# Output projection of a hybrid encoder layer as seven block products instead of eight, with split weight operands parked in DRAM

## The chip, the cores and the metric

The kernel runs on one core of one Trainium2 chip. Its time is the device time of one execution in microseconds (us). Five engines work side by side and meet at semaphores: TensorE (PE: matmuls and transposes), VectorE (DVE), ScalarE (ACT), GpSimd (POOL) and SyncE (SP). Transfers are issued from a queue of SP, ACT or POOL and are carried by sixteen DMA engines that all queues share. The tile framework orders each engine's instructions ahead of time; only TensorE's order is written out by hand in the stages described here.

## The reference

One layer of a bidirectional encoder: 512 tokens, model width 1024, float32.

```python
u = h @ w_in
z, xbc, dt_f_raw, dt_b_raw, q, k, v, gate_logits = jnp.split(u, ...)
y_ssd = ssd_branch(z, xbc, ...) @ w_proj_ssd        # (512, 2048) @ (2048, 1024)
y_att = attention_branch(q, k, v) @ w_proj_attn     # (512, 256) @ (256, 1024)
gates = jax.nn.sigmoid(gate_logits + b_gate).reshape(bsz, s, N_BRANCHES, D_MODEL)
mix = (gates[:, :, 0] * y_ssd + gates[:, :, 1] * y_att) @ w_out   # (512, 1024) @ (1024, 1024)
h = layer_norm(alpha * h + mix, ln1_g, ln1_b)
f = jnp.square(jax.nn.relu(h @ w_up)) @ w_down      # width 4096
h = layer_norm(alpha * h + f, ln2_g, ln2_b)
```

The change is about the product with `w_out`, and about what has to be ready around it.

## The kernel before

**Split operands.** Every float32 operand `r` of a large product is held as a high part `h` (a cast by ScalarE to the matmul type, line 109) and a low part `l = r - h` (a subtraction by VectorE, line 110). A product is then three matmuls into the same PSUM bank: high x high, high x low, low x high (`mm3`, lines 165 to 172).

**Weights.** `Stream` (lines 75 to 130) loads weight tiles of 128x1024 (512 KB) in the order of use into three raw buffers (`wraw`), from SP's queue, and splits each one just ahead of its use. A tile with a `hold` is split into a buffer of its own that stays (`wo` for the output projection, `wb` for the attention projection, `wu` for the first blocks of the up projection).

**Order of the stages.** The input projection and the scan over four groups of heads (to about 455 us); attention, with the first twelve half products of `w_proj_ssd` running between (to about 577 us); the last four half products, each followed by the attention projection and the gates of two blocks of 128 features (`proj_b`, lines 1072 to 1083, to 605 us); the output projection and the first norm (605 to 657 us); the up and down projections, already done as seven block products each; the last norm.

**The output projection.** `proj_b(d)` finishes the gated sum of feature block `d` for all 512 tokens and splits it into `mixh[d]` and `mixl[d]`. Eight PSUM banks hold the result: four token blocks of 128 by two column halves of 512. `out_mm(i, k, ...)` adds feature block `k` to token block `i`: two halves of three matmuls. Blocks `k` 0 to 3 run over all four token blocks with weights that stream in; `out_tail(i)` then does blocks 4 to 7 of one token block with the four tiles held in `wo`, adds the scaled input row `h1[i]` (two evictions, line 1182) and normalizes it (`layer_norm`, lines 1131 to 1140). While the later token blocks run, the finished ones are transposed for the up projection (`h1_transpose`). `up_first` is the first half of two up blocks and covers the norm of the last token block.

```python
    for k in range(4):
        w = ws.get(2)
...
        for i in range(4):
            out_mm(i, k, *w)
...
    out_tail(0)
    out_tail(1)
    out_tail(2)
    h1_transpose(0)
    out_tail(3)
```

**Buffers.** `yh`, `yl` (the split scan output) lie on the right side of the on-chip memory and are read until the last half product of `w_proj_ssd`; `h1` and what is allocated after it take their place. `wb` lies on the left side and is read until the last `proj_b`. A new buffer's first write waits for the last reader of what lay there.

Of the kernel before, what the change touches and what calls it, by code (L numbers as in the profile page):

```python
# [10 lines left out]
F32 = mybir.dt.float32  # L11
# [5 lines left out]
P = 128  # L17
# [29 lines left out]
def hybrid_layer_kernel(ctx: ExitStack, tc: tile.TileContext, t: dict, out: bass.AP):  # L47
# [18 lines left out]
    dr_w0 = dram.tile([S, 4], F32, name="dr_w0")  # L66

# [7 lines left out]
    class Stream:  # L75
        def __init__(self):
            self.srcs, self.raw, self.hl, self.n, self.end = [], {}, {}, 0, None

# [16 lines left out]
        def prep(self, i):  # L95
            if i < len(self.srcs) and i not in self.hl and (self.end is None or i < self.end):
                self.load(i)
                ap, width, hold = self.srcs[i]
                if hold and hold[0] not in held:
                    return  # L100
                r = self.raw[i]
                if hold:
                    h = held[hold[0]].tile([P, 1024], F32R, name=f"wh{i}", tag=f"h{hold[1]}", bufs=1)
                    l = held[hold[0]].tile([P, 1024], F32R, name=f"wl{i}", tag=f"l{hold[1]}", bufs=1)
                else:
                    h = wp.tile([P, 1024], F32R, name=f"wh{i}", tag="wh", bufs=2)
                    l = wp.tile([P, 1024], F32R, name=f"wl{i}", tag="wl", bufs=2)
                with tc.high_priority(PRIO):
                    a = act.copy(h[:, :width], r[:, :width])  # L109
                    v = dve.tensor_sub(l[:, :width], r[:, :width], f32(h[:, :width]))  # L110
# [510 lines left out]

    late = [None]
# [16 lines left out]
    def ssd(g):  # L639
# [104 lines left out]
        for pr in range(4):  # L744
# [14 lines left out]
            pool.tensor_add(be[:, 0, P:S - P], be[:, 0, P:S - P], be[:, 1, P:S - P])  # L759
# [57 lines left out]
    a_order = [(d, i) for i in range(2) for d in range(3)] + [(d, i) for d in range(3, 8) for i in range(2)]  # L817
    for n, (d, i) in enumerate(a_order):
        if n == 12:
            for q in range(2):  # L820
                ws.add(t["w_pa"][q], hold=("wb", q))
        ws.add(t["w_ps"][d, i])
        if n >= 12:
            ws.add(t["w_out"][n - 8], hold=("wo", n - 12))
    for k in range(4):
        ws.add(t["w_out"][k])
        if 0 < k <= NU:
            ws.add(t["w_up"][k - 1], hold=("wu", k - 1))
# [3 lines left out]
    mixa = [mx.tile([P, S], F32, name=f"mixa{d}", tag="mix", bufs=9) for d in range(8)]  # L832
    mixl = []
    ath = [mx.tile([P, S], F32R, name=f"ath{i}") for i in range(2)]
    atl = [mx.tile([P, S], F32R, name=f"atl{i}") for i in range(2)]
# [13 lines left out]
    aq = at_ctx.enter_context(tc.tile_pool(name="aq", bufs=1, side="right", reuse_waits="tile"))  # L849

    def attention():
# [21 lines left out]
        b12 = ap.tile([P, 8, P], F32, name="b12")  # L873
# [11 lines left out]
        b0 = aq.tile([P, 4, 256], F32, name="b0")  # L885
# [143 lines left out]
        def merge(i):  # L1029
# [3 lines left out]
            act.copy(ath[i], ac)  # L1033
            dve.tensor_sub(atl[i], ac, f32(ath[i]))

        todo = []
# [35 lines left out]
    def proj_b(d):  # L1072
# [7 lines left out]
        dve.tensor_add(gb, gb, mixa[d])  # L1080
        mixl.append(mx.tile([P, S], F32R, name=f"mixl{d}", tag="mix", bufs=9))
        act.copy(mixh[d], gb)
        dve.tensor_sub(mixl[d], gb, f32(mixh[d]))
# [9 lines left out]
    mixh = [mh.tile([P, S], F32R, name=f"mixh{d}") for d in range(8)]  # L1093
    held["wo"] = mp.enter_context(tc.tile_pool(name="wop", bufs=1, reuse_waits="tile"))
    wb_ctx = ExitStack()
    held["wb"] = wb_ctx.enter_context(tc.tile_pool(name="wbp", bufs=1, reuse_waits="tile"))
    wb = [ws.get() for _ in range(2)]
    wo, wu = [], []
    for d, i, bs in ((6, 0, (0, 1)), (6, 1, (2, 3)), (7, 0, (4, 5)), (7, 1, (6, 7))):
# [3 lines left out]
        for q in bs:  # L1103
            proj_b(q)
    wb_ctx.close()
    yp_ctx.close()
# [10 lines left out]
    hf_ctx = ExitStack()  # L1117
    hf = hf_ctx.enter_context(tc.tile_pool(name="hf", bufs=1, side="right", reuse_waits="tile")).tile([P, KT, S], F32, name="hf")
# [34 lines left out]
    pso_b = [(6, 7), (5, 2), (3, 4), (0, 1)]  # L1153
    pso_t = [bank(n, f"ps_o{n}") for n in range(8)]
    pso = [[pso_t[n] for n in b] for b in pso_b]

    def out_mm(i, k, wh, wl):
        ts_ = slice(i * P, (i + 1) * P)
        for c in range(2):
            cs = slice(c * 512, (c + 1) * 512)  # L1160
            mm3(pso[i][c], [(mixh[k][:, ts_], mixl[k][:, ts_])], [(wh[:, cs], wl[:, cs])], first=(k == 0), last=(k == KT - 1))
# [3 lines left out]
    for k in range(4):  # L1165
        w = ws.get(2)
        if 0 < k <= NU:
            wu.append(ws.get(1))
        for i in range(4):
            out_mm(i, k, *w)  # L1170
        if k == 0:
            g1 = load_ln(held["wu"], 0)
        dma.dma_start(h1[k], t["x"][k * P:(k + 1) * P, :])

    def out_tail(i):
        for k in range(4):
            out_mm(i, 4 + k, *wo[k])
            if i == 3 and k == 1:
                h1_transpose(1)
        for c in range(2):  # L1180
            cs = slice(c * 512, (c + 1) * 512)
            dve.scalar_tensor_tensor(h1[i][:, cs], h1[i][:, cs], 2.0 * ALPHA, pso[i][c], op0=ALU.mult, op1=ALU.add)
        layer_norm(h1[i], g1, 0, f"a{i}")
# [20 lines left out]
    def up_first(i):  # L1204
        pre.append(bank((6, 7, 5, 2)[i], f"ps_u0_{i}"))
# [26 lines left out]
    def up_block(ch, b):  # L1232
# [16 lines left out]
    LO, HI = slice(0, 256), slice(256, 512)  # L1249
# [408 lines left out]
def _layout(a):  # L1658
# [21 lines left out]
    o["w_out"] = c(a["w_out"].reshape(KT, P, D))  # L1680
# [21 lines left out]
```

## Time and profile before

| what | before |
|---|---|
| median of 3 runs | 985.0 us (984.65 to 985.14) |
| the profiled execution | 984.4 us, its span 982.7 us |
| TensorE busy | 972.9 us (99%) |
| VectorE busy | 806.5 us (82%) |
| ScalarE busy | 607.2 us (62%) |
| GpSimd busy | 76.2 us (8%) |
| moved by DMA | 155.94 MB, 159 GB/s over the span |
| granted TensorE clock | 0.999 |

The profile is one execution. The span runs from its first to its last instruction; times in its views are counted from the span's start. A row of the timeline gives the start, the duration, the engine, the line of the kernel, the operation and the names of the tiles, written tile first, and how many instructions are merged into the row; a bracket names the idle time before it and what ended it. A row of stretches gives, for each engine, the busy time and the number of instructions in it, then the granted clock, the mean busy share of the sixteen DMA engines, and GB/s. Matmul durations overlap, so a busy TensorE isn't a TensorE at its peak.

### The profile page before, as it was taken

What the parts mean: (1) busy time and instruction counts of PE and PEld (TensorE: products, weight loads), DVE (VectorE), ACT (ScalarE), POOL (GpSimd) and SP (SyncE); (2) the same over time, 40 slices, a digit from 0 to 9 for tenths busy, and PEclk for the clock granted to TensorE, in tenths of its full rate; (3) what the DMA queues carried; (4) which work ended last, traced back from release to release, by engine and by line L of the source; (5) the groups of instructions that cost most, each with busy time, mean ns of one, the idle gap of its engine ahead of it and who ended that gap; (6) DMA issues with size and microseconds to landing.
All of it is one profiled execution on the core that took longest, in us unless ns stands there. A gap on an engine that the chain in (4) does not pass through costs nothing.

```text
span 982.7 us, 14783 instructions
## 1 busy us (share of the span) xinstructions
PE 972.9 (99%) x5447; PEld 835.1 (85%) x5447; DVE 806.5 (82%) x1235; ACT 607.2 (62%) x1149; POOL 76.2 (8%) x79
## 2 busy tenths in 40 slices
PE   9999999999999999999999999999999999999997
PEld 6988888888888888788778888899989998989986
DVE  7986998798998899997798258498898898898757
ACT  6664796469856995694775344147666666656620
POOL 0100100120011101202000000000200110110000
PEclk9999999999999999999999999999999999999999
DMA  9666476335652485474773248313953854671322
GB/s 355 152 146 171 127 199 199 97 116 153 214 151 90 149 243 147 123 234 140 252 237 111 79 149 313 127 44 125 242 148 131 213 129 171 176 169 44 110 83 86
DMA packets 57992, 155.94 MB, mean 159 GB/s; under 512 B 7488, under 2 KB 10432, under 8 KB 57664
## 3 DMA queue, kind: packets, MB, share of 16 engines
q1 hardware_dynamic: 53072, 139.04, 43.9%
q0 software_dynamic: 4560, 15.44, 8.6%
q8 instruction: 43, 0.70, 0.3%
q10 hardware_dynamic: 288, 0.52, 0.1%
q14 instruction: 29, 0.24, 0.1%
HBM read 128.25 MB, written 12.44 MB: 143 GB/s over the span
## 4 chain that ended last, share of the span: by engine, by line
PE 86%; DVE 8%; ACT 3%; DMA 2%; issue 1%; DVEq 0%; SPq 0%; ACTq 0%
PE ps_pa L159 9%; PE ps_z L159 8%; PE ps_x L159 8%; PE ps_x L1341 8%; PE ps_z L1341 4%; PE ps_k L159 3%; PE ps_g L159 3%; PE ps_q L159 3%; PE ps_pX L169 2%; PE ps_pX L170 2%; PE ps_pX L171 2%; PE ps_y L1341 2%; PE ps_vX L351 2%; PE ps_u L159 2%; PE ps_pZ L169 2%; PE ps_pZ L170 2%
## 5 line engine op out<-in xcount | busy, mean ns | idle before, releaser
L110 DVE TENSOR_TENSOR wl<-wraw,wh 128x1024 fp32r<-128x1024 f32 x103 | 129.7, 1265 | 57.4 <-ACT wh L109 42.2
L109 ACT CAST wh<-wraw 128x1024 fp32r<-128x1024 f32 x103 | 107.2, 1045 | 73.9 <-PE ps_o L171 13.2
L1457 DVE TENSOR_TENSOR cl<-wq_B,ch 128x1024 fp32r<-128x1024 f32 x42 | 51.2, 1220 | 14.8 <-ACT ch L1456 14.3
L1456 ACT CAST ch<-wq_B 128x1024 fp32r<-128x1024 f32 x42 | 44.1, 1050 | 24.0 <-PE ps_pX L171 16.6
L159 PE MATMUL ps_pa<-yh,wh 128*128 128x512 f32 x128 | 51.7, 404 | 0.0
L1425 POOL DMA_DIRECT2D wq_B<-wq_B x24 | 20.6, 856 | 391.2 <-DMA wq_B<-in_w_dn_dram 225.4
L159 PE MATMUL ps_g<-xh,wh 128*128 128x512 f32 x128 | 50.6, 396 | 0.0
L159 PE MATMUL ps_z<-xh,wh 128*128 128x512 f32 x128 | 50.4, 393 | 0.0
L159 PE MATMUL ps_g<-xl,wh 128*128 128x512 f32 x128 | 49.9, 390 | 0.0
L159 PE MATMUL ps_z<-xl,wh 128*128 128x512 f32 x128 | 49.9, 389 | 0.0
L159 PE MATMUL ps_pa<-yl,wh 128*128 128x512 f32 x128 | 48.4, 393 | 0.0
L724 ACT ACTIVATE U<-bc,acr 128x128 f32<-128x128 f32 x128 | 42.3, 391 | 8.9 <-DMA bc<-dr_acr 7.7
L159 PE MATMUL ps_x<-xh,wh 128*128 128x512 f32 x120 | 47.2, 394 | 0.0
L159 PE MATMUL ps_x<-xl,wh 128*128 128x512 f32 x120 | 46.7, 389 | 0.0
L522 DVE SCALAR_TENSOR_TENSOR acc<-ps_x,vec,acc 128x510 f32<-128x510 f32 (+1 forms) x60 | 44.5, 742 | 0.7 <-ACT acc L520 0.3
L726 DVE SCALAR_TENSOR_TENSOR U<-bc,acr,U 128x128 f32<-128x128 f32 x128 | 43.2, 375 | 0.8 <-ACT U L724 0.8
L730 ACT ACTIVATE G<-cb,tok 128x128 f32<-128x128 f32 x128 | 41.7, 391 | 0.0
L169 PE MATMUL ps_pX<-ch,ah 128*128 128x512 f32 x96 | 37.6, 392 | 0.0
L170 PE MATMUL ps_pX<-cl,ah 128*128 128x512 f32 x96 | 37.6, 392 | 0.0
L171 PE MATMUL ps_pX<-ch,al 128*128 128x512 f32 x96 | 37.3, 389 | 0.0
L1450 ACT CAST ah<-r 128x1024 fp32r<-128x1024 f32 x21 | 22.1, 1053 | 20.6 <-PE ps_pX L170 14.3
L159 PE MATMUL ps_pa<-yh,wl 128*128 128x512 f32 x128 | 34.8, 392 | 0.0
(884 smaller groups left out, 2841.2 us busy)
## 6 DMA issues: line engine op xcount, KB each, us to landing
wraw<-in_w_in_dram SPq DMA_DIRECT2D x66, 512.0 KB, 3.8
bc<-dr_acr SPq DMA_DIRECT2D x64, 256.0 KB, 4.4
pr<-in_w_up_dram SPq DMA_DIRECT2D x28, 512.0 KB, 5.5
wq_B<-in_w_dn_dram SPq DMA_DIRECT2D x24, 512.0 KB, 4.5
wq_B<-wq_B POOLq DMA_DIRECT2D x24, 512.0 KB, 4.7
be<-dr_ear SPq DMA_DIRECT2D x32, 256.0 KB, 5.1
wraw<-in_w_ps_dram SPq DMA_DIRECT2D x16, 512.0 KB, 4.2
dr_gate<-g SPq DMA_DIRECT2D x16, 256.0 KB, 2.8
```

Of the source, the lines that this page charges most:

```text
L109: a = act.copy(h[:, :width], r[:, :width])
L110: v = dve.tensor_sub(l[:, :width], r[:, :width], f32(h[:, :width]))
L159: ins = pe.matmul(ps, l, r, start=(first and n == 0), stop=(last and n == len(seq) - 1))
L169: pe.matmul(ps, lh, rh, start=(first and i == 0), stop=False, skip_group_check=not check)
L170: pe.matmul(ps, lh, rl, start=False, stop=False, skip_group_check=not check)
L171: ins = pe.matmul(ps, ll, rh, start=False, stop=(last and i == n - 1), skip_group_check=not check)
L522: dve.scalar_tensor_tensor(acc[:, o0:o1], ps[:, i0:i1], w(k), acc[:, o0:o1], op0=ALU.mult, op1=ALU.add)
L724: act.activation(U[:, ch(c)], bb[:, ch(c)], AF.Identity, bias=acr[:, c, 32 + h:33 + h])
L726: dve.scalar_tensor_tensor(U[:, ch(c)], bf[:, ch(c)], acr[:, c, h:h + 1], U[:, ch(c)], op0=ALU.subtract, op1=ALU.min)
L1341: pe.matmul(ps[:, LO], w_[:, wk], src[:, x, k0 + k, cs], start=(first and i == 0), stop=(i == 11), skip_group_check=not first)
L1456: act.copy(h, w[:, j, :])
L1457: dve.tensor_sub(l, w[:, j, :], f32(h))
```

## The change

The 512x1024 gated sum and the 1024x1024 weights are each cut into two by two blocks (`a11` to `a22`, `b11` to `b22`; an activation block is 256 tokens by 512 features, a weight block 512 by 512), and the result is put together from seven block products, in the order 1, 2, 5, 3, 6, 7, 4.

- **Weights.** Products 1 and 2 use weight blocks as they are; they come through the stream and are held in `wo`. Product 3 uses a block as it is. Products 5, 7 and 6 use sums of two or three blocks: `out_sums` makes these in DRAM (`dr_sum`), by copies and accumulating transfers from POOL's queue, one step behind the sum of `be` in each step from `j` = 8 on, in the last two groups of the scan. Product 4 uses `dr_sum[6]` plus a fourth block: it is added in the buffer `t4` and split there by ScalarE and VectorE.
- **Parking.** The operands of 3, 5, 7 and 6 are split in sixteen blocks of 128x512: loaded, cast, subtracted, and both parts stored to `dr_op` (512 KB a block, 2 MB an operand). Twelve blocks run during attention, behind chosen weight splits; four (those of 6) run between the last `proj_b`, in the buffers `wsq`. The operands are read back from POOL's queue: 5 into `w5p` (where `wsq` lay), 3 into `w3p` (where `wb` lay), 6 and 7 into the `wo` buffers of products 1 and 2.
- **Activations.** The gated sum stays in float32 (`mix`). `proj_b` splits its first 256 tokens for products 1 and 2. `out_split` splits the operands of 5, 3, 6, 7 and 4, with four sums and differences on VectorE in between.
- **Results.** Each product is 24 matmuls into two banks; `out_evict` adds them to `h1`, fourteen times in all instead of eight. The norm's statistics follow the last eviction of each half row. Token blocks 0 and 1 are complete after product 6, 2 and 3 after product 4.
- **Names and layout.** The list `mix` of the scan is now `tasks`; `w_out` is handed over in another layout.

```diff
+    dr_sum = {p: dram.tile([2, P, 1024], F32, name=f"dr_sum{p}") for p in (5, 7, 6)}
+    dr_op = {p: dram.tile([4, P, 2, 512], F32R, name=f"dr_op{p}") for p in (5, 3, 6, 7)}
...
+    def out_sums():
+        w = t["w_out"]
+        for p, first, second in ((5, w[0, 0:2], w[1, 0:2]), (7, w[1, 0:2], w[1, 2:4]), (6, dr_sum[5], w[1, 2:4])):
+            pool.dma_start(dr_sum[p], first, max_dma_last_dim=4096)
+            yield
+            pool.dma_start(dr_sum[p], second, accum_op=ALU.add, max_dma_last_dim=4096)
+            yield
...
-            pool.tensor_add(be[:, 0, P:S - P], be[:, 0, P:S - P], be[:, 1, P:S - P])
+            be_sum = pool.tensor_add(be[:, 0, P:S - P], be[:, 0, P:S - P], be[:, 1, P:S - P])
+            if j >= 8:
+                with tc.issue_after(be_sum.ins):
+                    next(w_sums, None)
...
+    SP_BLOCKS = [(p, k) for p in (3, 5, 7, 6) for k in range(4)]
...
+            home, tag, bufs = (late_wsp[0], "sp", 4) if n >= 12 else ((wsp, "sp", 2), (wsp, "sp", 2), (aq, "b0", 1), (ap, "b12", 1))[n % 4]
+            sp_tiles[n] = home.tile([P, 2, 512], F32R, name=f"sp{p}{k}", tag=tag, bufs=bufs)
+            dma.dma_start(f32(sp_tiles[n][:, 1, :]), src[k // 2, :, (k % 2) * 512:(k % 2 + 1) * 512])
+
+    def spill(n):
+        p, k = SP_BLOCKS[n]
+        r = sp_tiles[n]
+        act.copy(r[:, 0, :], f32(r[:, 1, :]))
+        dve.tensor_sub(r[:, 1, :], f32(r[:, 1, :]), f32(r[:, 0, :]))
+        pool.dma_start(dr_op[p][k], r)
+        spill_load(n + 4)
...
     with tc.manual_schedule(engines={mybir.EngineType.PE}):
         run(attention(), proj_bg(a_order[:12]), 73.0, 48 * QT)
+    for n in range(12):
+        a, v = ws.prepped[first_a + (8, 9, 11)[n // 4]]
+        with tc.issue_after(a.ins), tc.issue_after(v.ins):
+            spill(n)
...
-            proj_b(q)
+            made = proj_b(q)
+        if (d, i) in ((6, 1), (7, 0)):
+            with tc.issue_after(made[0].ins), tc.issue_after(made[1].ins):
+                for n in range(2):
+                    spill(12 + 2 * (d - 6) + n)
...
+    def whole_load(pool_, p):
+        w = whole(pool_, p)
+        for k in range(4):
+            pool.dma_start(w[:, :, k, :], dr_op[p][k])
...
+    w3p = mp.enter_context(tc.tile_pool(name="w3p", bufs=1, reuse_waits="tile"))
+    w5_ctx = ExitStack()
+    whole_load(w5_ctx.enter_context(tc.tile_pool(name="w5p", bufs=1, reuse_waits="tile")), 5)
+    whole_load(w3p, 3)
...
+    for j in range(2):
+        dma.dma_start(t4[:, j, :], t["w_out"][0, 2 + j])
+        pool.dma_start(t4[:, j, :], dr_sum[6][j], accum_op=ALU.add)
...
+    def out_mm(p, q):
+        name, rows, c, sign = O_OUTS[p]
+        first = p in (1, 2, 5)
...
+        for k in range(4):
+            mm3(ps, [(aop[p][0][:, k, ts_], aop[p][1][:, k, ts_])], [wop[p][k]], first=(first and k == 0), last=(k == 3), check=first)
+            yield
...
+    def w_tiles(p, n):
+        w = [[wopp.tile([P, 1024], F32R, name=f"wo{p}{x}{j}", tag=f"{x}{n + j}", bufs=1) for x in "hl"] for j in range(2)]
+        for j in range(2):
+            for x in range(2):
+                pool.dma_start(w[j][x].rearrange("p (k n) -> p k n", k=2), dr_op[p][2 * j:2 * j + 2, :, x, :].rearrange("k p n -> p k n"))
...
+    dve.tensor_sub(a21, a21, a22)
+    out_split(5)
+    dve.tensor_sub(a21, a21, a11)
+    dve.tensor_add(a12, a12, a21)
+    o_gate = product_out(1)
+    w_tiles(6, 0)
+    out_split(3)
+    product_out(2, True)
+    w_tiles(7, 2)
+    product_out(5)
+    out_split(6)
+    dve.scalar_tensor_tensor(a11, a21, -1.0, a22, op0=ALU.mult, op1=ALU.subtract)
+    product_out(3)
+    w4 = whole(w3p, 4)
...
+    out_split(7)
+    drain(out_mm(6, 0))
+    out_evict(6, 0, True)
+    layer_norm(h1[0], g1, 0, "a0")
+    drain(out_mm(6, 1))
+    out_evict(6, 1, True)
+    layer_norm(h1[1], g1, 0, "a1")
+    wu.append(ws.get(1))
+    out_split(4)
+    product_out(7, True)
...
+    drain(out_mm(4, 0))
+    out_evict(4, 0, True)
+    layer_norm(h1[2], g1, 0, "a2")
     h1_transpose(0)
+    last_out = out_mm(4, 1)
+    drain(last_out, 2)
+    h1_transpose(1)
+    drain(last_out)
+    out_evict(4, 1, True)
+    layer_norm(h1[3], g1, 0, "a3")
+    drain(up_first(0))
     h1_transpose(2)
```

More of the change, by code (lines that the diff above doesn't have):

```diff
@@ L823, in hybrid_layer_kernel @@
         if n >= 12:
[L824 to L828, printed above, removed]
+            ws.add(t["w_out"][0, n - 12], hold=("wo", n - 12))
+    for k in range(NU):
+        ws.add(t["w_up"][k], hold=("wu", k))
     mp = ExitStack()
     mx = mp.enter_context(tc.tile_pool(name="mx", bufs=1, reuse_waits="tile"))
[L832 to L835, printed above, removed]
+    mix = mx.tile([P, KT, S], F32, name="mix")
+    mixa = [mix[:, d, :] for d in range(KT)]
+    at_h = mx.tile([P, 2, S], F32R, name="at_h", tag="at_h", bufs=1)
+    at_l = mx.tile([P, 2, S], F32R, name="at_l", tag="at_l", bufs=1)
+    ath, atl = [at_h[:, i, :] for i in range(2)], [at_l[:, i, :] for i in range(2)]
     yhp = yp_ctx.enter_context(tc.tile_pool(name="yhp", bufs=1, side="right", reuse_waits="tile"))
@@ L1032, in merge @@
             dve.tensor_add(ac, ac, pn[i])
-            act.copy(ath[i], ac)
-            dve.tensor_sub(atl[i], ac, f32(ath[i]))
+            a = act.copy(ath[i], ac)
+            merged[i] = a, dve.tensor_sub(atl[i], ac, f32(ath[i]))
+        for n in range(4):
+            spill_load(n)
         todo = []
@@ L1079, in proj_b @@
         dve.scalar_tensor_tensor(gb, gb, 1.0, ps, op0=ALU.add, op1=ALU.mult)
[L1080 to L1083, printed above, removed]
+        dve.tensor_add(mixa[d], gb, mixa[d])
+        o = aop[1 if d < 4 else 2]
+        a = act.copy(o[0][:, d % 4], mixa[d][:, :256])
+        return a, dve.tensor_sub(o[1][:, d % 4], mixa[d][:, :256], f32(o[0][:, d % 4]))
     def proj_bg(order):
@@ L1151, in bank @@
         return pw.tile([P, 512], F32, name=name, tag=f"b{n}", bufs=1)
[L1153 to L1161, printed above, removed]
+    LO, HI = slice(0, 256), slice(256, 512)
@@ new lines, in out_mm, with out_evict @@
+    def out_mm(p, q):
+        name, rows, c, sign = O_OUTS[p]
+        first = p in (1, 2, 5)
+        if first:
+            o_ps[name, q] = bank(O_BANKS[name][q], f"ps_o{p}{q}")
+        ps = o_ps[name, q]
+        ts_ = slice(q * P, (q + 1) * P)
+        for k in range(4):
+            mm3(ps, [(aop[p][0][:, k, ts_], aop[p][1][:, k, ts_])], [wop[p][k]], first=(first and k == 0), last=(k == 3), check=first)
+            yield
+    def out_evict(p, q, last=False):
+        name, rows, c, sign = O_OUTS[p]
+        i = rows * 2 + q
+        ps = o_ps[name, q]
+        h = h1[i][:, c * 512:(c + 1) * 512]
+        with tc.high_priority(PRIO):
+            if (i, c) in o_seen:
+                ins = dve.tensor_tensor(h, h, ps, op=ALU.add if sign > 0 else ALU.subtract)
+            else:
+                o_seen.add((i, c))
+                ins = dve.scalar_tensor_tensor(h, h, 2.0 * ALPHA, ps, op0=ALU.mult, op1=ALU.add)
+            if last:
+                dve.bn_stats(st2[i][:, c, :], h)
+        return ins
@@ L1163, in hybrid_layer_kernel @@
+    product_out(3)
+    w4 = whole(w3p, 4)
+    for j in range(2):
+        ks = slice(2 * j, 2 * j + 2)
+        flat = lambda x: w4[:, x, ks].rearrange("p k n -> p (k n)")
+        act.copy(flat(0), t4[:, j, :])
+        dve.tensor_sub(flat(1), t4[:, j, :], f32(flat(0)))
+    w5_ctx.close()
+    t4_ctx.close()
+    hf_ctx = ExitStack()
+    hf = hf_ctx.enter_context(tc.tile_pool(name="hf", bufs=1, side="right", reuse_waits="tile")).tile([P, KT, S], F32, name="hf")
     wu_ctx = ExitStack()
     held["wu"] = wu_ctx.enter_context(tc.tile_pool(name="wu", bufs=1, side="right", reuse_waits="tile"))
[L1165 to L1183, printed above, removed]
+    g1 = load_ln(held["wu"], 0)
+    out_split(7)
+    drain(out_mm(6, 0))
+    out_evict(6, 0, True)
+    layer_norm(h1[0], g1, 0, "a0")
@@ L1185, in h1_transpose @@
+    drain(out_mm(6, 1))
[4 more added lines that the diff above has]
+    product_out(7, True)
+    with tc.issue_after(o_gate.ins):
+        wu.append(ws.get(1))
     def h1_transpose(i):
```

108 lines of the change are left out of this document (79 added, 29 removed).

## The prediction

> **What bounds the kernel now.** First the page: the busy shares and the chain that ended last.
>
> ```profile
> span 982.7 us, 14783 instructions
> PE 972.9 (99%) x5447; PEld 835.1 (85%) x5447; DVE 806.5 (82%) x1235; ACT 607.2 (62%) x1149; POOL 76.2 (8%) x79
> ...
> PE 86%; DVE 8%; ACT 3%; DMA 2%; issue 1%; DVEq 0%; SPq 0%; ACTq 0%
> ```
>
> TensorE carries the chain. Matmuls overlap, so what one costs is the step between two starts, not its duration. Next, therefore, the list of the output projection's instructions and the timeline of TensorE there:
>
> ```profile
> L171 PE MATMUL ps_o<-wh,mixl x64: 388/389/393, 605.9 to 650.8; 128*128 128x512 f32 x64
> ...
> 605.43 0.39 PE L169 MATMUL ps_o<-wh,mixh 128*128 128x512 f32 x1
> ...
> 609.79 0.39 PE L169 MATMUL ps_o<-wh,mixh 128*128 128x512 f32 x1
> ...
> 623.16 0.39 PE L171 MATMUL ps_o<-wh,mixl 128*128 128x512 f32 x1
> ...
> 643.80 1.03 PE L1190 MATMUL ps_ht<-ident,h 128*128 128x128 f32 x8
> 644.59 0.48 PE L169 MATMUL ps_o<-wh,mixh 128*128 128x512 f32 x1
> ...
> 651.02 0.28 PE L159 MATMUL ps_u<-ht,wh 128*128 128x256 f32 x1
> ```
>
> From 609.79 to 623.16 there are 60 matmuls, 59 steps: 13.37 / 59 = 0.227 us each, although each lasts 0.389. The stage has 3 x 64 = 192 of them, 43.5 us, and two groups of eight transposes of 0.79 us (643.80 to 644.59). 605.43 + 43.5 + 1.6 = 650.5, and the next stage's first matmul starts at 651.02: TensorE waits for next to nothing, so any new wait goes onto the time in full.
>
> Then the stretches, for what the others have free, and the issues on POOL's timeline that fall into the last one:
>
> ```profile
> core 0: us, PE busy (x) PEld busy (x) DVE busy (x) ACT busy (x) POOL busy (x), PEclk, DMA share, GB/s
> 540.00:577.00 37.00, 37.00 (x272) 29.61 (x271) 9.54 (x11) 14.67 (x24) 0.00 (x0) 1.00 0.22 71
> 577.00:602.70 25.70, 25.70 (x115) 21.27 (x114) 21.36 (x27) 10.94 (x15) 0.00 (x0) 1.00 0.81 257
> 608.00:616.00 8.00, 8.00 (x37) 6.61 (x36) 4.99 (x6) 3.56 (x4) 0.00 (x0) 1.00 0.99 391
> 609.00:613.00 4.00, 4.00 (x20) 3.30 (x19) 3.24 (x4) 3.40 (x4) 0.00 (x0) 1.00 1.04 427
> 773.40:778.90 5.50, 5.50 (x48) 5.50 (x48) 5.43 (x8) 5.23 (x10) 0.86 (x1) 1.00 1.03 199
> ...
> 772.00 0.86 POOL L1425 DMA_DIRECT2D wq_B<-wq_B  x1 [3.86 <-DMA wq_B<-wq_B]
> 773.60 0.86 POOL L1425 DMA_DIRECT2D wq_B<-wq_B  x1 [0.74 <-DVE cl L1457]
> ```
>
> The reader is to see two prices. At 608 to 616 the sixteen DMA engines are full and move 391 GB/s: 512 KB (524,288 bytes) takes 1.34 us of all of them. In the last stretch two accumulating transfers of 512 KB fill them for 5.5 us: 2.7 us each, twice a plain one. And from 577 on they are 0.81 busy already.
>
> **The change part by part.**
>
> *Matmuls.* Seven products of 2 row blocks x 4 k x 3 = 24 make 168 instead of 192. 24 x 0.227 = 5.4 us less, all on the path. The sixteen transposes stay.
>
> *Sums of weights in DRAM.* Six 1 MB transfers from POOL in the scan's last two groups, three of them accumulating: 3 x 2.7 + 3 x 5.4 = 24 us of the engines in some 200 us. Behind them on POOL's queue stand state products, squares and sums of `be`, the next `be` sum 11 us off. The rows that could come late are those ScalarE reads in this stage:
>
> ```profile
> L724 ACT ACTIVATE U<-bc,acr 128x128 f32<-128x128 f32 x128 | 42.3, 391 | 8.9 <-DMA bc<-dr_acr 7.7 <-DVE acc L522 1.1
> ...
> 300.00:380.00 80.00, 79.90 (x383) 66.70 (x381) 73.63 (x126) 64.36 (x146) 7.38 (x7) 1.00 0.59 174
> ...
> 430.99 0.79 POOL L759 TENSOR_TENSOR be<-be 128x256 f32<-128x256 f32 x1 [12.98 <-DVE be L758]
> 442.20 0.73 POOL L759 TENSOR_TENSOR be<-be 128x256 f32<-128x256 f32 x1 [10.43 <-DVE be L758]
> ```
>
> They wait 7.7 us in all of 128 now, with the DMA 0.59 busy and TensorE at 79.90 of 80, so such waits don't reach it. I take 0; bounds 0 and +1.5 (a fifth more waiting, passed on whole). A gain has no source.
>
> *Twelve parked blocks in attention.* Each: a 256 KB load, a cast and a subtraction of 128x512, a 512 KB store. The stretch 540 to 577 has VectorE 9.5 of 37 busy, ScalarE 14.7, the DMA 0.22. The blocks add 12 x 0.69 = 8.3 us to VectorE (the price of line 1083 below), about as much to ScalarE, and 12 x 1.34 x 1.5 = 24 us to the DMA: it fits. I take 0. A cast that reaches ScalarE's queue ahead of its load would hold the copies of the transposed scores behind it, which TensorE needs; bounds 0 and +2.
>
> *Reloading the parked operands.* Here I come out against the change. High and low parts make 2 MB per product, sixteen 512 KB transfers for products 5, 3, 6 and 7, all on POOL's queue. What else must pass at the same time:
>
> ```profile
> 601.84 0.42 SPq L1173 DMA_DIRECT2D h<-in_x_dram  x1
> 603.82 0.42 SPq L1173 DMA_DIRECT2D h<-in_x_dram  x1
> 604.93 0.33 SPq L88 DMA_DIRECT2D wraw<-in_w_up_dram  x1
> 605.32 0.90 SPq L1173 DMA_DIRECT2D h<-in_x_dram  x2
> 606.26 0.45 SPq L1122 DMA_DIRECT2D ln<-in_ln_dram  x1
> ...
> 602.71 0.39 PE L169 MATMUL ps_pb<-ath,wh 128*128 128x512 f32 x1
> ...
> 602.73 0.69 DVE L1083 TENSOR_TENSOR mixl<-gb,mixh 128x512 fp32r<-128x512 f32 x1 [0.69 <-ACT mixh L1082]
> ```
>
> The rows of x (`h1`, four), the norm's weights (1 MB, two units) and a `w_up` tile stay; the change adds two loads and two accumulations for `t4`. `t4` lies where `yh` and `yl` lie, read until 602.7. Nor can the parked operands start early: product 5's buffer takes the place of the last four parked blocks, two of which are split behind the sixth gate's subtraction (602.73) and then stored, so it is free at about 608 by estimate (602.7, four instructions of 0.7, a store of 1.34 and its landing); product 3's takes the place of the attention weights, in use to 605.4; 6 and 7 take the buffers of products 1 and 2. On POOL's queue a load that waits holds all behind it, `t4`'s additions and products 6 and 7 too.
>
> From 602.7, in units of 512 KB: x 4, norm 2, `w_up` 1, `t4` 2, two stores 2, parked operands 16: 27 x 1.34 = 36.2 us. Two accumulations: 5.4 us. Sum 41.6 us with the engines never idle: product 7's last quarter lands at 644.3.
>
> When is it wanted? Product 1 starts at 605.4, each takes 24 x 0.227 = 5.44, so 7 starts at 632.6 and reads its last quarter nine matmuls on: 634.7. TensorE waits 644.3 - 634.7 = **9.6 us**, spread over products 5, 3, 6 and 7, and each quarter that arrives is used up in 0.7 us, so later work doesn't win it back. Bounds: nothing waited (all of it hidden), and about 12 (the POOL queue idle until 608 and nothing but x moving before).
>
> The page "DMA: Bandwidth & Descriptors" of the Trainium skill, in "Issuing engines are not separate DMA queues", says that transfers issued from different engines end up on the same sixteen DMA engines and interleave. Here the 0.99 share at 391 GB/s arises from SP's queue alone, and no row shows POOL loading beside it at full rate; by that rule POOL's reloads get no bandwidth of their own.
>
> *VectorE in the stage.* Durations from the groups of 605.4 to 651:
>
> ```profile
> L110 DVE TENSOR_TENSOR wl<-wraw,wh 128x1024 fp32r<-128x1024 f32 x6 | 7.2, 1222 | 12.6 <-ACT wh L109 12.6
> L1182 DVE SCALAR_TENSOR_TENSOR h<-h,ps_o 128x512 f32<-128x512 f32 x6 | 4.1, 687 | 2.4 <-PE ps_o L171 2.4
> ...
> 605.40:629.90 24.50, 11.10 (x13) 1.00 0.65 240
> 629.90:651.00 21.10, 18.18 (x29) 1.00 0.09 26
> ```
>
> Now 29.3 us of 45.6. Added: five splits of activation sums and four sums at 1.22 (11.0), six more evictions at 0.69 (4.1), two splits for product 4 (2.4). Removed: four weight splits (4.9). That makes 41.9 us. With the waits the stage lasts 39.7 + 9.6 = 49 us, so it is hidden; without them 41.9 stands against 39.7, and it is not (second rival). The first-layer norm gets lighter per row (one eviction and one statistic at the end instead of two) but starts later for rows 0 and 1: I take 0, bounds -0.5 and +2.
>
> *Sum.* -5.4 + 9.6 = +4.2 us. The profiled execution took 984.4 us (span 982.7 and 1.7 around it), 0.6 under the median of 985.0. 984.4 + 4.2 = **988.6 us**.
>
> **Rivals.**
>
> *A: the reloads are hidden, VectorE takes part back.* This one ends on the other side. It needs w7 landed by 634.7, so 9.6 us of the 41.6 gone by then: x, norm and `w_up` (7 units, 9.4 us) would have to pass before 602.7. For it: the stage from 577 to 602.7 leaves 0.19 x 25.7 = 4.9 us free. Against: in the rows above the x loads start at 601.84. VectorE is then 2.2 us short (41.9 against 39.7): 984.4 - 5.4 + 2.2 = 981.2.
>
> *B: half hidden.* At the rate of 609 to 613, 427 GB/s, a unit takes 1.23 us: 27 x 1.23 + 5.4 = 38.6, landing at 641.3, a wait of 6.6, and 984.4 - 5.4 + 6.6 = 985.6. For it: the rate was reached, and some x rows may move earlier. Against: it held for 4 us only. The page named above gives in "Anatomy of one DMA" a fit of 2.0 us plus bytes over 436 GB/s; by it a unit is 1.20 us and the estimate 984.8, this same rival.
>
> *C: the clock.* If one of the waits is long and whole rather than in pieces, TensorE may restart slow. What slow means is in the first matmuls of the run:
>
> ```profile
> 1.19 4.02 PE L234 MATMUL ps_warm<-warm 128*128 128x512 bf16 x9 [1.19 <-DVE warm L231]
> ```
>
> Nine in 4.02 us, about 0.43 us a step instead of 0.23. Two such spells of some 4 us cost 2 us each: 988.6 + 4 = 992.6. Against: each quarter brings work every 1.3 to 2.7 us. The page "TensorE: Matmul & The Clock Gate", in "Part 1", says that an idle window of about 3.4 us halves the clock; this trace has no idle stretch to show it on.
>
> **How the numbers follow.** The forecast (wait over 8 us, slower) 0.42; C, or attention holding TensorE up beside it, 0.08; B 0.18; A 0.32. The same for faster, within and slower: 0.2% is 2 us, about what a measurement of this kernel can tell from no change; under 983.0 lies A (0.32), from 983.0 to 987.0 B (0.18), above it the rest (0.50). The range leaves out A's best part (no VectorE loss, 979.0) and C's end: 980.5 to 992.5. The forecast's own range is 987 to 991 (waits of 8 to 12).
>
> **What would show it.** Right: matmul count of the output products 168; DMA share near 1.0 from about 603 to 640; TensorE idle before products 5, 3, 6 or 7 with a transfer from `dr_op` as releaser, about 9.6 us in all; VectorE with gaps in the stage. A instead: no such waits, VectorE without gaps to the last norm, and the wait before the fourth group of transposes. C: a granted clock under 1.00 in the stage. Wrong in its place: new TensorE waits between 540 and 577, or longer waits for `bc`. The weakest step is the ledger's start at 602.7: each unit that passes before it takes 1.34 us off the time.

## The result, and the profile after

| | before | after |
|---|---|---|
| median | 985.06 us (984.65 to 985.14, 4 runs) | 1058.55 us (1056.45 to 1060.53, 4 runs) |
| profiled execution, its span | 984.4 us, 982.7 us | 1057.2 us, 1055.4 us |
| attention starts (first `ps_s`) | 485.0 | 540.1 |
| output projection starts (first `ps_o`) | 605.4 | 662.1 |
| up projection starts (first `ps_u`) | 651.0 | 721.3 |

The ratio is 1.0747 (95% interval 1.0721 to 1.0772): slower, as forecast, but by 73 us instead of 4. The starts in the table, read off TensorE's timeline, say where it went. Of 72.7 us of span, 55.1 are lost before attention, 1.6 between there and the output projection, 13.6 in the output projection (59.2 us instead of 45.6) and 2.4 behind it.

The page of the changed kernel:

```profile
span 1055.4 us, 14919 instructions
...
PE 987.5 (94%) x5423; PEld 839.4 (80%) x5423; DVE 822.0 (78%) x1264; ACT 619.0 (59%) x1168; POOL 101.7 (10%) x119
...
PE 40%; DMA 6%; DVE 3%; issue 1%; ACT 0%; POOL 0%; DVEq 0%; SPq 0%; POOLq 0%; ACTq 0%
...
L737 ACT ACTIVATE U<-bc,acr 128x128 f32<-128x128 f32 x128 | 42.1, 390 | 17.5 <-DMA bc<-dr_acr 16.0
```

TensorE has 24 instructions fewer, as it should, and is busy 94% instead of 99%. The waits for `bc` grew from 7.7 to 16.0 us. That is not 55, so the next view is what TensorE waited for from 300 to 540 us (who waits, for whom: us in total, times, longest):

```profile
PE ps_st L173 <- DVE x L612: 20.4, 1, 20.4
PE ps_ms L593 <- ACT sqh L582: 6.4, 1, 6.4
PE ps_g L163 <- ACT wh L112: 5.8, 1, 5.8
PE ps_y L608 <- DVE x L612: 4.7, 2, 2.4
PE ps_st L173 <- ACT U L741: 3.9, 1, 3.9
```

The clock is part of the 55 us too. It was granted at half speed in five spells of this stretch, 44.4 us in all; the longest, 20.5 us from 421.0, lies in this row:

```profile
416.00:452.00 36.00, 11.74 (x29) 9.03 (x30) 25.95 (x72) 23.58 (x68) 4.57 (x4) 0.62 0.41 124
```

The eight waits of over 1 us add up to 43.8 us; in 21.7 us of the halved spells TensorE was at work, which by estimate costs half of that, 10.8 us. Together that is 54.6 of the 55.1 us.

The longest wait is for VectorE, for an addition into `x`. What feeds `x` is the fold of `be` (line 776), for which POOL sums the two directions of `be` (line 772). POOL's timeline, then VectorE's:

```profile
338.12 1.65 POOL L772 TENSOR_TENSOR be<-be 128x256 f32<-128x256 f32 x1 [8.48 <-DVE be L771]
356.11 0.74 POOL L772 TENSOR_TENSOR be<-be 128x256 f32<-128x256 f32 x1 [16.34 <-DVE be L771]
356.79 0.61 POOL L629 DMA_DIRECT2D dr_sum<-in_w_out_dram  x1
357.39 0.97 POOL L631 DMA_DIRECT2D dr_sum<-in_w_out_dram  x1
399.51 0.73 POOL L772 TENSOR_TENSOR be<-be 128x256 f32<-128x256 f32 x1 [41.15 <-DVE be L771]
```

```profile
355.56 0.42 DVE L771 TENSOR_TENSOR be<-be,ps_yo 128x256 f32<-128x256 f32 x1
...
392.49 1.41 DVE L776 SCALAR_TENSOR_TENSOR x<-x,vec,be 128x512 f32<-128x512 f32 x2
...
398.96 0.41 DVE L771 TENSOR_TENSOR be<-be,ps_yo 128x256 f32<-128x256 f32 x1
...
434.75 0.75 DVE L776 SCALAR_TENSOR_TENSOR x<-x,vec,be 128x512 f32<-128x512 f32 x1
```

The second sum of this view is ready at 356.9; POOL then issues two transfers in 0.6 and 1.0 us and is free again: its queue is not held. VectorE folds that sum at 392.5, with no wait in brackets: the fold simply stands that late in VectorE's order. Before, the same fold came 1.4 us behind its product:

```profile
354.03 0.41 DVE L758 TENSOR_TENSOR be<-be,ps_yo 128x256 f32<-128x256 f32 x1
...
355.39 0.74 DVE L760 SCALAR_TENSOR_TENSOR x<-x,vec,be 128x512 f32<-128x512 f32 x1
```

The order written into the two kernels, by row numbers (repeats of a line on one tile make one row), for the pairs of heads 9 to 11 (lines 758 and 760 before are 771 and 776 after):

```
before  395 L758 be   398 L760 x<-x,vec,be     417 L758   419 L760     436 L758   438 L760
after   395 L771 be   454 L776 x<-x,vec,be     417 L771   455 L776     462 L771   498 L776
```

59, 38 and 36 rows behind the product that it needs, instead of 3, 2 and 2; counted as single instructions in the traces it is 71, 45 and 60 instead of 3 each time. VectorE, ScalarE, POOL and SP are ordered by the tile framework. That it puts the readers of POOL's sums so late is what one would see if it held POOL to be busy with a transfer of 2 x 128 x 1024 for tens of microseconds; this reason is inferred, and no run shows it.

In the output projection (the stretches, then TensorE's timeline):

```profile
662.10:673.00 10.90, 10.90 (x48) 8.91 (x48) 10.59 (x14) 2.92 (x4) 0.95 (x2) 1.00 0.99 348
673.00:692.00 19.00, 14.50 (x50) 10.39 (x48) 11.54 (x14) 5.27 (x6) 11.21 (x16) 0.82 1.10 317
692.00:701.00 9.00, 1.07 (x2) 0.59 (x3) 2.99 (x3) 3.99 (x4) 0.70 (x1) 0.61 1.12 398
701.00:721.30 20.30, 19.71 (x87) 15.89 (x87) 15.64 (x25) 3.95 (x10) 0.00 (x0) 0.92 0.37 122
```

```profile
677.57 0.76 PE L173 MATMUL ps_o<-wo,oh 128*128 128x512 f32 x1 [4.32 <-DMA wo<-dr_op]
...
696.83 0.77 PE L173 MATMUL ps_o<-wo6h,oh 128*128 128x512 f32 x1 [4.93 <-DMA wo6h<-dr_op]
700.70 0.79 PE L174 MATMUL ps_o<-wo6l,oh 128*128 128x512 f32 x1 [3.10 <-DMA wo6l<-dr_op]
```

The DMA engines are full until 701, and three waits for reloads make 12.35 us. The granted clock is 0.82 and 0.61 in the two stretches with waits: in the halved spells 21 steps from one matmul to the next took 0.43 to 0.71 us, 9.8 us in all, where 21 x 0.227 = 4.8 would do: 5.0 us more.

### The profile page after: what moved, and what is told of

Same layout as the page of the kernel before. It is cut to its first block, busy times and chain, and to the rows that moved or that the text cites. A ratio compares the mean times of both kernels' runs of the same rounds, so it can differ in the third digit from the quotient of the medians.

```text
span 1055.4 us, 14919 instructions
## 1 busy us (share of the span) xinstructions
PE 987.5 (94%) x5423; PEld 839.4 (80%) x5423; DVE 822.0 (78%) x1264; ACT 619.0 (59%) x1168; POOL 101.7 (10%) x119
## 3 DMA queue, kind: packets, MB, share of 16 engines
q0 software_dynamic: 13136, 39.56, 16.3%
## 4 chain that ended last, share of the span: by engine, by line
PE 40%; DMA 6%; DVE 3%; issue 1%; ACT 0%; POOL 0%; DVEq 0%; SPq 0%; POOLq 0%; ACTq 0%
PE ps_x L1498 8%; PE ps_pa L163 6%; PE ps_z L1498 4%; PE ps_pX L175 2%; PE ps_pX L173 2%; PE ps_pX L174 2%; PE ps_u L163 2%; PE ps_y L1498 2%; DMA wo6l<-dr_op 2%; DMA dr_op<-sp 2%; PE ps_pZ L175 2%; PE ps_pZ L174 2%; PE ps_pZ L173 2%; PE ps_d L173 1%; PE ps_d L175 1%; PE ps_d L174 1%
## 5 line engine op out<-in xcount | busy, mean ns | idle before, releaser
L113 DVE TENSOR_TENSOR wl<-wraw,wh 128x1024 fp32r<-128x1024 f32 x99 | 123.8, 1254 | 55.4 <-ACT wh L112 33.2
L112 ACT CAST wh<-wraw 128x1024 fp32r<-128x1024 f32 x99 | 103.0, 1046 | 85.1 <-PE ps_g L163 26.7
L1614 DVE TENSOR_TENSOR cl<-wq_B,ch 128x1024 fp32r<-128x1024 f32 x42 | 51.3, 1220 | 15.9 <-ACT ch L1613 15.9
L163 PE MATMUL ps_g<-xh,wh 128*128 128x512 f32 x128 | 55.2, 431 | 5.8 <-ACT wh L112 5.8
L163 PE MATMUL ps_g<-xl,wh 128*128 128x512 f32 x128 | 53.8, 420 | 0.0
L163 PE MATMUL ps_x<-xl,wh 128*128 128x512 f32 x120 | 46.8, 390 | 0.0
L163 PEld LDWEIGHTS ps_g<-xh,wh 128*128 128x128 f32 x128 | 26.9, 210 | 12.4 <-ACT wh L112 6.2
L772 POOL TENSOR_TENSOR be<-be 128x256 f32<-128x256 f32 x16 | 14.0, 875 | 218.5 <-DVE be L771 203.5
```

What stands on the lines that cost most here:

```text
L163: ins = pe.matmul(ps, l, r, start=(first and n == 0), stop=(last and n == len(seq) - 1))
L1614: dve.tensor_sub(l, w[:, j, :], f32(h))
```

## The experiments

Theory 1: the order of the other engines, disturbed by the way the sums are written, costs most of the scan. Theory 2: the transfers of the sums crowd the loads of `bc` and `be`. Theory 3: POOL's queue is held on the chip. For the output projection: the ledger of bytes, against the place of POOL's queue and against VectorE.

| run | time, us | ratio to before (95%) | attention starts | output projection, length | span |
|---|---|---|---|---|---|
| b1_sums_only | 1037.4 (one time) | | 538.3 | 45.3 | 1035.6 |
| b2_sp_copies | 1043.6 (one time) | | 544.4 | 45.3 | 1041.8 |
| r1_flat_rows | 1016.6 | 1.0283 to 1.0332 | 499.9 | 60.4 | 1017.2 |
| e1_halves | 1014.3 | 1.0278 to 1.0313 | 497.4 | 58.7 | 1012.6 |
| e6_behind_decays | 1003.1 | 1.0170 to 1.0205 | 486.5 | 58.1 | 1000.5 |
| e5_late_up_loads | 1004.5 | 1.0175 to 1.0212 | 486.3 | 60.4 | 1003.0 |
| e3_no_reload_67 | 1003.8 (one time) | | 497.9 | 46.8 | 1002.0 |
| e7_t4_in_dram | 999.1 | 1.0120 to 1.0155 | 486.6 | 53.4 | 997.3 |
| e9_p6_not_parked | 994.4 | 1.0066 to 1.0112 | 487.6 | 48.4 | 994.2 |
| e10_p67_not_parked | 995.7 | 1.0087 to 1.0140 | 490.2 | 52.1 | 997.1 |
| e11_gated_pairs | 994.5 | 1.0076 to 1.0118 | 486.0 | 45.0 | 991.0 |
| e13_t4_last | 989.0 | 1.0028 to 1.0056 | 486.3 | 42.7 | 987.0 |

### The sums alone (b1_sums_only)

```diff
 (kernel before)
-            pool.tensor_add(be[:, 0, P:S - P], ...)
+            be_sum = pool.tensor_add(be[:, 0, P:S - P], ...)
+            if j >= 8:
+                with tc.issue_after(be_sum.ins):
+                    next(w_sums, None)      # the six transfers, as in the change
```

> The kernel before, with the six 1 MB transfers of the weight sums added on POOL in the same places (nobody reads them); output projection as before. All three theories: the loss in the scan alone, attention at about 540 us, about 985 + 53 = 1038 us. If instead the loss needs the rest of the change (the parked blocks, the new memory layout), about 985 to 990.

1037.4 us, attention at 538.3: the six transfers alone make 53.3 of the 55.1 us that the scan loses. The parked blocks and the new buffers are not needed for it.

### The same bytes written otherwise (e1_halves, r1_flat_rows)

The edits are shortened here and below.

```diff
 e1:
-            pool.dma_start(dr_sum[p], first, ...)
+            for h in range(2):
+                pool.dma_start(dr_sum[p][h], first[h], ...)      # the second one likewise, two behind each be sum
 r1:
-            pool.dma_start(dr_sum[p], first, ...)
+            pool.dma_start(dr_sum[p].rearrange("h p n -> (h p) n"), first.rearrange("h p n -> (h p) n"), ...)
```

> Each 1 MB transfer of the weight sums is issued as two of 512 KB, at the same place behind the same be sum, on the same queue, with the same bytes. Theory 1 (the order: the instruction that folds be into x stands 59, 38 and 36 rows behind the last be product in VectorE's order for heads 9, 10 and 11, against 1 to 4 rows in the kernel before; with halves it stands 2 to 3 rows behind): the scan comes back, attention starts at about 485 instead of 540 us, TensorE has no wait of 20 us at 395 to 416, and the time falls by about 55 to 1000 to 1006 us. Theory 2 (the transfers crowd the loads of bc and be) and theory 3 (POOL's queue is held on the chip while the transfers run): bytes and queue are the same, so about 1058 us, attention at about 540.

> The changed kernel with one edit: the six transfers of the weight sums stay whole (1 MB each, same bytes, place and queue), but both sides are written as 256 rows of 1024 instead of 2 x 128 x 1024. With that the instruction that folds be into x stands 1 to 3 rows behind the be product again in VectorE's order, and the orders of TensorE, VectorE, ScalarE and SP are row for row those of the run with halves. Theory 1 (the order costs the scan 44 us): attention starts at about 497, the time is 1014 +- 3 us. Rival (a transfer of 1 MB holds something that two of 512 KB do not): as the changed kernel, 1058 us.

1014.3 and 1016.6 us: 44 and 42 us come back. r1 is the clean one. It moves the same 1 MB pieces on the same queue, in as many packets (13136 on POOL's queue) and with the same landing time (9.2 us in the median, 9.1 in the changed kernel); TensorE's order is the same row for row. What differs is the order of the other engines. Of VectorE's 1264 instructions 197 stand elsewhere. POOL's order differs too: the changed kernel issues the second and third transfer together at 356.8 and 357.4, r1 issues one behind each sum. In r1 the wait of 20.4 us is gone. Its VectorE timeline:

```profile
341.83 0.75 DVE L776 SCALAR_TENSOR_TENSOR x<-x,vec,be 128x512 f32<-128x512 f32 x1
...
360.73 0.74 DVE L776 SCALAR_TENSOR_TENSOR x<-x,vec,be 128x512 f32<-128x512 f32 x1
...
376.02 0.74 DVE L776 SCALAR_TENSOR_TENSOR x<-x,vec,be 128x512 f32<-128x512 f32 x1
```

Theory 1 is shown, for the order of the engines taken together, and with it the rival that the size of a transfer matters falls. r1 is within its 1014 +- 3 us; e1 missed its range of 1000 to 1006, because attention still starts 12 to 15 us late. The 42 us hold some 6 us of halved clock by estimate: in the scan r1 has 10.2 us of halved spells left, where the changed kernel had 44.4.

### Where the sums stand (e6_behind_decays, b2_sp_copies)

```diff
 e6 (from e1):
-            if j >= 8:
-                with tc.issue_after(be_sum.ins): ...             # two halves
+                decay = pool.tensor_mul(h3(pv), h3(prev[d, c]), ...)
+                if g >= 1:
+                    with tc.issue_after(decay.ins):
+                        next(w_sums, None)                       # one half behind each
```

> As the run with halves, but the twelve 512 KB transfers of the sums are issued one behind each of POOL's twelve decays of the scan state (groups 2 to 4, near 203 to 214, 298 to 310 and 394 to 405 us), where the DMA engines were 0.2 to 0.4 busy, instead of behind the sums of be, where they were 0.7 to 0.9 busy. VectorE's order is the same row for row. If the 12.4 us that the run with halves still loses in the scan are contention with the loads of bc (ScalarE waits 2.2 and 5.9 us for bc there): attention starts at 485 to 487 us instead of 497.4, and the time is 1002 +- 2 us. If POOL's queue is held by the transfers: the decays feed the state products and come late, so no gain, 1014 or more.

Attention at 486.5, 1003.1 us: 11 us back, as theory 2 says. VectorE's order is that of e1 row for row. ScalarE's wait for `bc` from 300 us to attention, in e1 and in e6 (it is 6.0 us before), and a stretch in which e1 loses about 3 of its 12 us, e1 and then e6:

```profile
ACT U L743 <- DMA bc<-dr_acr: 16.6, 7, 5.9
```

```profile
ACT U L743 <- DMA bc<-dr_acr: 5.9, 6, 3.5
```

```profile
330.00:360.00 30.00, 28.76 (x139) 23.74 (x137) 23.28 (x46) 23.44 (x64) 3.63 (x4) 1.00 0.90 250
```

```profile
330.00:360.00 30.00, 30.00 (x146) 25.27 (x145) 28.43 (x55) 28.38 (x77) 3.00 (x2) 1.00 0.70 205
```

So theories 1 and 2 both hold, 42 to 44 us and 11. Theory 3 falls: the decays behind which the transfers now stand feed the state products, and nothing came late.

> The kernel before, with six 1 MB transfers at the same places, but issued on SP's queue and as plain copies without accumulation (nobody reads them). POOL's queue holds none of them. Theory 1 (the order, which follows from what POOL is taken to be busy with): about the time before, 985 to 988 us. Theory 2 (traffic beside the loads of bc and be): still slower by 20 us or more, since half or more of the traffic is still there. Theory 3 (POOL's queue held on the chip): about 985 to 988 too; the run with halves tells 1 from 3.

1043.6 us, but this run did not test what it was meant to. Freed from POOL, the copies were put early into SP's queue (issued from 19.8 to 267.3 us), and the loss lies there: TensorE waits for weight splits, 42.6 us in three lines.

```profile
PE ps_x L160 <- ACT wh L110: 16.3, 1, 16.3
PE ps_z L160 <- ACT wh L110: 15.4, 3, 7.6
PE ps_C L160 <- ACT wh L110: 10.9, 1, 10.9
```

What share of that is traffic and what is SP's order (VectorE's and ScalarE's orders were disturbed here too) is left open; it says only that moving such transfers to SP is no way round.

### The ledger of the output projection (e3, e7, e5)

```diff
 e3 (from e1):
-    w_tiles(6, 0)
+    wop[6] = wop[1]                                   # products 6 and 7 use the weights of 1 and 2
-    w_tiles(7, 2)
+    wop[7] = wop[2]
 e7 (from e6):
-        dma.dma_start(t4[:, j, :], t["w_out"][0, 2 + j])
-        pool.dma_start(t4[:, j, :], dr_sum[6][j], accum_op=ALU.add)
+        dma.dma_start(t4[:, j, :], dr_sum[4][j])      # finished in DRAM in the scan
```

> As the run with halves, but products 6 and 7 use the weights of products 1 and 2 that lie in their buffers, so eight of the sixteen 512 KB reloads are left out. Ledger: 10.7 us less, product 6 no longer waits (9.1 us of waits and about 2.5 us of halved clock gone), the wait of 4 us before product 5 stays, since it hangs on the parked stores: the output projection falls from 58.7 to about 47 us, the time from 1014.3 to about 1002.5. If the total of bytes is not what counts, product 6 or 4 waits again elsewhere and less than 5 us are won.

> As the run behind the decays, and product 4's weight sum is finished in DRAM too (four more transfers of 512 KB, behind the decays of the first group on), so that t4 is loaded plainly instead of by two loads and two accumulating transfers in the output projection. By the ledger 5.4 us of accumulation leave the busy window: product 6's waits fall from 9.1 to about 4, the time is about 997. If accumulation costs the window nothing beyond its bytes, 2.7 us: about 999.5. If the four transfers disturb the scan, that shows in the start of attention (later than in the run behind the decays).

e3 leaves out eight reloads, so its result is not that of the layer. Its stage falls from 58.7 to 46.8 us (expected 47), and the one long wait left is that before product 5, 4.41 us. With the reloads gone the stage gets shorter by what the ledger says. e7: the stage falls from 58.1 to 53.4, 4.7 us (5.4 by the ledger), but the time only from 1003.1 to 999.1, 4.0 us. Expected were 997, or 999.5 if accumulation costs nothing beyond its bytes: the time lies at this rival, the stage nearer to the ledger, and the run does not tell them apart.

> As the run behind the decays, and the first loads of the up projection's weight pairs (three of 512 KB, issued at 644 us in the run with halves, in the middle of the reloads for products 6 and 7) wait for the first eviction of product 6. If the output projection's waits follow the ledger of bytes, 3 x 1.34 = 4 us less lie ahead of product 6's weights: its waits (5.7 + 3.4 us) fall to about 5, and the time is 3 to 5 us under the run behind the decays, about 998. If the waits come from where POOL's queue stood (9 us behind the parked stores), the gate changes nothing, about 1002.

No answer: the loads went out at 632.3 us, 632.2 without the edit, and every engine's order is the same, so the kernel is the same on the chip. 1004.5 against 1003.1 us, and a stage of 60.4 against 58.1, is then what two such runs differ by; a smaller difference of time or of stage between two rows of the table says nothing.

### What is not parked need not come back (e9, e10, e11)

```diff
 e9 (from e7):
-    SP_BLOCKS = [(p, k) for p in (3, 5, 7, 6) for k in range(4)]
+    SP_BLOCKS = [(p, k) for p in (3, 5, 7) for k in range(4)]
+                pool.dma_start(f32(w[j][1]), dr_sum[6][j])       # in w_tiles(6, 0)
+                act.copy(w[j][0], f32(w[j][1]))
+                dve.tensor_sub(w[j][1], f32(w[j][1]), f32(w[j][0]))
 e10: product 7 in the same way
 e11 (from e9):
+            if n < 2:
+                pool.tensor_mul(raw_w[n, j][:, 0:1], st2[0][:, 1, 0:1], st2[0][:, 1, 0:1])
             dma.dma_start(raw_w[n, j], t["w_up"][ch * 8 + b + j])
```

> As the run with t4 made in DRAM, but product 6 is not parked: its f32 sum (two loads of 512 KB instead of four) is loaded into the buffer of the low parts and split there by ScalarE and VectorE. The last four parked stores, which landed 10 to 12 us after their issue and held product 5's first loads, are gone. Ledger: 4 + 2 units fewer, 8 us; the waits before product 5 (5.8 us) go to 0 to 1, those before product 7 (4.2 us) to about 1, and 2 us of halved clock with them: the output projection falls from 53.4 to 43 to 45 us, the time from 999 to 989 to 991. Rival (VectorE, 2.4 us more work in a stage where it then has 44 us to do): the stage stays at 46 or more, 992 or above, with VectorE lacking gaps.

> As the run before, and product 7 likewise: 2 units fewer in the window (2.7 us), four stores and four loads fewer in attention, 2.4 us more on VectorE. If bytes still set the end: another 1 to 2 us, 988. If VectorE sets it: slower than the run before by 1 to 3 us, 991 to 994.

> As the run with product 6 not parked, and the first three loads of weight pairs for the up projection (4 us of the DMA engines) start only behind the statistics of product 6's first row block, made so by a data dependency (the attempt before changed no issue time: they went out at 632.3 us with and without it). Ledger: if product 7 still waits in the run before, up to 1 us less; if it does not, no change within 0.2 %, or a loss of 1 us where the up projection then waits for the pairs.

e9: 994.4 us, the stage 48.4 instead of 53.4; half of what I expected. Product 5's loads now go out at 573.7 and nobody waits for them. But a new wait of 4.7 us stands before product 3, and this is ScalarE's timeline there:

```profile
626.30 1.04 ACT L1285 CAST wo6h<-wo6l 128x1024 fp32r<-128x1024 f32 x1 [6.84 <-DMA wo6l<-dr_sum]
627.59 1.04 ACT L1285 CAST wo6h<-wo6l 128x1024 fp32r<-128x1024 f32 x1 [0.24 <-DMA wo6l<-dr_sum]
628.54 1.04 ACT L1240 CAST oh<-mix 128x1024 fp32r<-128x1024 f32 x1
```

ScalarE waits 6.84 us at the cast of product 6's weights, and behind it in its queue stands the split of product 3's activations: a load that is late for a later product holds an earlier one. e10 is no gain: 1.3 us over e9, with runs that overlap. A wait of 3.58 us before product 3 is left, and TensorE now also waits 1.53 and 2.76 us for VectorE's splits of `ol`, as its rival had it; the stage is 52.1. e11 is e9 to 0.1 us in the median; its profiled execution has the stage at 45.0, but then TensorE loses 2 us near 729, which fits pairs that came later (it was not taken apart).

### The transfers that nobody needs yet (e13_t4_last)

```diff
 (from e9)
-    for j in range(2):
-        dma.dma_start(t4[:, j, :], dr_sum[4][j])
 ...
     w_tiles(7, 2)
+    with tc.issue_after(w_last[0].ins):               # product 7's last reload
+        for j in range(2):
+            pool.dma_start(t4[:, j, :], dr_sum[4][j])
```

> As the run with product 6 not parked, but t4's two loads (2.7 us of the DMA engines) are issued from POOL's queue behind product 7's reloads instead of from SP's in the middle of the rows of x; the other engines' orders are the same row for row. Product 4 is the last to need them. Ledger: product 3's weights, for which TensorE waited 4.9 us with 6.8 us of halved clock behind it, land 2.7 us earlier: that wait falls to about 2, the halved clock may go (another 3 us), and the time falls from 994.4 to 989 to 992. If the two loads cost the reloads nothing, 994.

989.0 us, 5.3 less, as expected; the way is not quite the one I wrote. What was late was not product 3's weights but the cast above, and it now runs at 621.60 instead of 626.30 (1.1 us of that because the stage starts earlier). TensorE's wait falls to 1.21 us, no halved clock is left, and the stage is 42.7 us: 2.9 under before. What holds it now is VectorE, without a gap for the last 23 us:

```profile
608.70:651.40 42.70, 40.44 (x186) 33.05 (x185) 40.90 (x54) 17.65 (x24) 7.80 (x12) 1.00 0.73 262
628.00:651.40 23.40, 22.35 (x107) 18.34 (x107) 23.40 (x32) 9.02 (x15) 0.00 (x0) 1.00 0.40 152
```

This is the best version found. It is still 0.3 to 0.6% over before: 1.3 us in the scan, 2.0 to the start of the output projection, 3.9 behind it, against 2.9 won.

## Why the prediction was wrong, step by step

- *Matmuls, -5.4*: right; 168 of them, and the step is 0.227 to 0.228 us where the clock is full.
- *Sums of weights, 0, bounds 0 and +1.5*: this is the step that failed; the scan lost 55.1 us. It asked whether the DMA engines and POOL's queue had room, and missed that an added instruction also changes the order in which the other engines' instructions are written. That cost 42 us (r1 against the changed kernel), with the clock that the long waits halved. What was asked was answered too low as well: the crowding of `bc` cost 11 us (e6 against e1), since the 0.59 that I quoted for 300 to 380 is a mean, and the sums of `be` stand in its busier part. Of the signs named for being wrong, the longer waits for `bc` came. Two stretches of the kernel before:

```profile
277.00:330.00 53.00, 52.90 (x300) 44.23 (x299) 45.95 (x65) 34.82 (x64) 10.20 (x8) 1.00 0.33 107
330.00:360.00 30.00, 30.00 (x147) 25.31 (x146) 28.15 (x55) 28.07 (x76) 2.40 (x2) 1.00 0.72 205
```

- *Parked blocks, 0, bounds 0 and +2*: within bounds; attention to the output projection took 122.0 instead of 120.4 us.
- *Reloading, +9.6*: the mechanism held, the number was partly luck. 41.6 us from the ledger's start (602.7 then, 659.4 with the 56.7 us of delay) gives 701.0, and the last wait for a reload ended at 700.70. But the ledger's 701.0 was for product 7's last quarter, and the load that TensorE waited for was product 6's; product 7's last quarter was issued at 692.25 and landed 15.9 us later, at 708.2. The price per unit held (e3), the list was short: the first three loads of weight pairs for the up projection (4.0 us) went out ahead of it, and a third parked store landed behind 659.4. With these 31 units the ledger gives 706.3. The wait came out at 12.35, just over the upper bound of 12.

```profile
686.98 4.87 SPq L1438 DMA_DIRECT2D pr<-in_w_up_dram  x3
692.25 0.70 POOL L1291 DMA_DIRECT2D wo7l<-dr_op  x1 [2.57 <-DMA t<-dr_sum]
```

The estimate that product 5's buffer is free 5 us after the last gate was off: its parked stores were issued from 652.4 to 661.7, and POOL got past them only at 672.49, 13 us after the ledger's start. At that time the DMA engines were full (0.99 from 662.1 to 673.0) and also carried the rows of x and `t4` from SP's queue. The page "DMA: Bandwidth & Descriptors" of the Trainium skill says in "Issuing engines are not separate DMA queues" that transfers issued from different engines run on the same sixteen DMA engines and interleave; the trace agrees, with a wait of 9.95 us on POOL.

```profile
660.52 1.14 POOL L886 DMA_DIRECT2D dr_op<-sp  x2 [7.02 <-DVE sp L885]
661.82 0.72 POOL L1162 DMA_DIRECT2D wo<-dr_op  x1 [0.16 <-issue]
672.49 4.90 POOL L1162 DMA_DIRECT2D wo<-dr_op  x7 [9.95 <-DMA dr_op<-sp]
```

- *Rival C, the clock, +4*: it came, at 5.0 us; I had given it 0.08. The waits are not in small pieces, they are two of over 4 us and one of 3.10. It came in the scan as well, where the prediction did not look for it (10.8 us by the estimate above). The page "TensorE: Matmul & The Clock Gate" of the Trainium skill, in "Part 1", puts the idle window that halves the clock at about 3.4 us. The length of one wait does not decide it in the runs here: the clock was halved behind waits of 2.91 us (e7) and 2.30 us (r1), and stayed full behind 2.82 us (e1), 3.49 us (e11) and 1.21 and 1.05 us (e13). The first row is r1's, the second e11's:

```profile
356.20:359.60 3.40, 3.40 (x10) 2.65 (x9) 1.27 (x4) 3.40 (x11) 0.00 (x0) 0.50 0.86 321
624.40:635.00 10.60, 7.11 (x32) 5.90 (x32) 10.60 (x12) 7.39 (x8) 0.00 (x0) 1.00 0.78 272
```

- *VectorE, 41.9 us of work*: 40.75 measured from 662.1 to 721.3. It was hidden, as forecast, behind the longer waits; e13, a kernel with other transfers, shows it as the bound once they are gone, which is rival A's condition. The stage is then 2.9 us shorter, where rival A had 3.2; its 981.2 was not reached because 7.2 us are lost outside the stage.
- The stage as a whole: -5.4 + 12.35 + 5.0 = 11.95 of the 13.6 us measured; the other 1.65 were not taken apart.
- *Behind the stage, 0*: 2.4 us were lost, 0.4 over the bound of +2 given for the first norm; 2.1 of them are the longer step of the up projection's matmuls (last section), which the sum did not have.

## What to carry to other kernels

Where a framework orders the engines, an added instruction costs twice: by what it does on the chip, and by what it does to the order of the others. Compare the order of every engine before and after, and look for the same instruction at another distance from its operand; an instruction that starts late with no wait shown is the sign of it, and writing the same transfer in another form undid it here. A share of the DMA engines averaged over a stage hides the stretches that matter: background transfers belong behind instructions that run where the engines are empty. And transfers that are needed last should be issued last, since a queue that stands behind one of them holds work for the next product too.

## What was not expected of the hardware

- The three waits for reloads cost about two fifths as much again (5.0 us on 12.35): the clock was halved for 6.8 us (from 677.0) and 10.2 us (from 694.1) in the changed kernel's stage, and the steps there were 0.43 us.
- The up projection's 504 matmuls of `ps_pX` and `ps_pZ` step by 0.2325 us in the changed kernel, by 0.2284 before, at full clock: 2.1 us. All kernels with the seven products have 0.2325; b1 and b2, which only add the transfers, have 0.2284. The instructions have the same shapes; where their operands lie on the chip may differ. The cause was not tried and stays open.
